# Two steps of a half product taken together per tile, and later transposes of queries and keys, in a two-layer encoder

## The chip, the cores and the metric

The kernel runs on one core of one Trainium2 chip. The metric is the device time of one execution in microseconds (us). Engines are named as the profile names them: PE is the matrix engine (PEld its weight loads), DVE the vector engine, ACT the scalar engine, POOL the GpSimd engine, SP the engine that here only issues transfers. Each engine takes its own instructions in their order and waits on semaphores for the others.

## The reference

The input is 512 tokens of width 1024. Two layers follow one another. Each normalises its input, multiplies it by one wide matrix, applies an attention with 16 heads of 64, multiplies the result by silu of a gate path and by an output matrix, and adds it to its input.

```python
def reference(x, norm_gain, a_w_in, ...):
    for i in range(DEPTH):                      # 2
        hn = rms_norm(x, norm_gain[i])
        j = i // N_MIXERS
        if i % N_MIXERS == 0:
            y = mixer_a(hn, a_w_in[j], ...)     # layer A
        else:
            y = mixer_b(hn, b_w_in[j], ...)     # layer B
        x = x + y.astype(x.dtype)
    return x

def mixer_a(hn, w_in, w_out, q_gain, k_gain, t5_bias):
    proj = hn @ w_in                            # q, k, v of three groups, and the gate
    for g, (window, dilation) in enumerate(DILATED_PAIRS):
        q = rms_norm(qkv[:, :, g, 0], q_gain[g])
        k = rms_norm(qkv[:, :, g, 1], k_gain[g])
        o, lse = dilated_group_attention(q, k, qkv[:, :, g, 2], ...)
    alpha = jax.nn.softmax(jnp.stack(lses), axis=0)
    y = jnp.sum(alpha[..., None] * jnp.stack(outs), axis=0)
    return (y * jax.nn.silu(gate)) @ w_out
```

Layer A attends in three groups of windows: every token, every 4th and every 16th. Layer B attends in a neighbourhood on a grid of 8 by 64. The change touches layer A alone.

## The kernel before

**Number format.** A factor of a large product is split into a high and a low part, and each step of a product is three matmuls into the same accumulator (`mm3`): high by high, high by low, low by high. In the profile the normalised input is `hn_h` and `hn_l`, the weights `wh` and `wl`.

**Weights.** They are read in a fixed order by transfers (`wraw`, issued by SP and POOL, into 8 buffers). ACT casts each piece of 512 columns to `wh` (6 buffers), POOL or DVE subtracts it to get `wl` (5 buffers); some pieces are first sums of two weight blocks, made by DVE. The generator `steps` hands out a pair `wh`, `wl` per step of a product.

**Chunks.** Layer A runs over 8 chunks hc = 0 to 7 of two heads. From hc=1 on, the queries, keys and values of a chunk come out of seven products of half size (`main_a`) in place of eight: both the tokens and the inner dimension are halved, and four of the seven work on sums and differences, prepared once, of the input (`mix_h`, `mix_l`). One such product (`product`) has KH = 4 steps of the inner dimension and two tiles i = 0, 1 of 128 tokens, each with an accumulator of its own of 128 by 512; in each step it does tile 0's three matmuls and then tile 1's. After the last step of a tile its `evac` reads the accumulator: `put22` subtracts that of the fourth mixed product from `rawq` on DVE. The order in a chunk is: two products on the plain input, with the gate of the chunk before in between; the values of the chunk before (from hc=2 on); four mixed products, n = 0, 1, 3, 2; the normalisation of the raw queries (`normed`); in hc=1 the values of chunk 0; and last a product on the plain input (`put21`) that adds on to the accumulators of the mixed product n=2. So this last product may write a tile only after DVE has read it in `put22`.

**Attention.** The attention of chunk hc is done while the products of the next chunk run. `q_a` transposes `rawq` by PE in four groups of four (first one that makes the keys `k0h`, `k0l`, then the queries `q0h`, `q0l`, then two for `q12`), `k_a` does two groups of `rawk` (for `k12`); ACT and DVE copy each group out of a bank. `attn_a` then computes scores in two halves (`scores(0)`, `scores(1)`, four banks each, in the profile `log`), DVE takes their minima into `p` and `mn`, ACT the exponentials, DVE and transfers (`pt`) transpose them, and `weigh` multiplies them by the values (`o`). The transposes and the scores share four banks, which are used in turn.

**What sets the order.** PE's order is that of the program text as it is generated: `run` draws a matmul group from the main generator (the products) and, when a model clock of PE's own time has passed the time named by the last `yield`, a piece from the side generator (the attention). A number yielded there is a pause in model nanoseconds before the next side piece. The first products of a chunk also carry keys such as `("scored", hc - 1)`, at which the main generator lets the side work run until that point is reached. `chore` slips halves of silu, on DVE, into the steps of products. The orders on DVE, ACT and POOL are set by a scheduler, and may change where PE's order does.

Of the kernel before, what the change touches and what calls it, by code (L numbers as in the profile page):

```python
# [22 lines left out]
P = 128  # L23
# [9 lines left out]
H = S // 2  # L33
KH = KT // 2
# [13 lines left out]
def tile_hybrid_encoder(  # L48
# [284 lines left out]
    def mm3(o, lh, ll, rh, rl, first, last, **kw):  # L333
        matmul(o, lh, rh, start=first, stop=False, **kw)
        matmul(o, lh, rl, start=False, stop=False, **kw)
        matmul(o, ll, rh, start=False, stop=last, **kw)
# [21 lines left out]
    def chore(now):  # L358

        if now and chores and next(chores[0], "end") == "end":  # L360
            chores.pop(0)

    def product(acc, stat, open_, evac, guard=None):


        if open_:
            acc += [ps_acc.tile([P, 512], F32, tag="acc", name="acc") for _ in range(2)]
        for k in range(KH):
            chore(1 <= k < KH - 1)
            if k == KH - 1:  # L370
                yield guard
            h, l = next(wsteps)
            for i in range(2):
                sh, sl = (t[:, P * i : P * i + P] for t in stat(k))
                mm3(acc[i], sh, sl, h, l, open_ and k == 0, k == KH - 1, skip_group_check=True)
                if k == KH - 1:
                    evac(i, acc[i])
                yield

    def project(stat_h, stat_l, n, evac, guard, need=None, after=None):  # L380

# [121 lines left out]
    wsteps = steps()  # L503
    wsteps = chain([next(wsteps)], wsteps)
# [198 lines left out]
    def main_a(hc):  # L703
# [49 lines left out]
            yield from v0_a(hc - 1, ("scored", hc - 1))  # L753
        for n, acc, first, put in ((0, c, True, put_v), (1, b, True, put_u), (3, c, False, put12), (2, b, False, put22)):
            yield "mix", n
            yield from product(acc, mixed(n), first, put, ("q", hc - 1) if n == 0 else None)
        normed(box[2], box[1], 8, "rawq", hc)
        if hc == 1:
            yield from v0_a(hc - 1)
        yield from product(b, hn(KH, H), False, put21)  # L760
        if hc == NHC - 1:
            st["y_h"] = big.tile([P, KT, S], F32R, tag="yh", name="y_h")
            st["y_l"] = big.tile([P, KT, S], F32R, tag="yl", name="y_l")
# [194 lines left out]
    def attn_a(hc):  # L958
# [192 lines left out]
        if hc < NHC - 2:  # L1151
            send = lambda: tc.keep_in_program_order(syn.dma_start(y_d[:, hc, :], gt))
            later_on(3000, send)
            stamp["w", hc] = 0
            yield
            if fill:
                later_on(1500, fill)
            yield 1500
            yield from q_a(hc + 1)
            return  # L1160
        st["tail"], back = y_back(range(2), "tr")
# [392 lines left out]
```

## Time and profile before

| | |
|---|---|
| runs | 835.29, 837.63 and 836.27 us |
| their median | 836.27 us |
| the profiled execution | 834.38 us |
| its span | 832.6 us |
| clock granted to PE over the span | 1.00 |
| PE busy | 820.4 us, 99% |
| DVE, ACT, POOL busy | 629.3, 506.3, 301.1 us |

The span is the time between the first and the last instruction on the profile. A line of a timeline gives start, length, engine, program line, operation, output and inputs, shapes, and the number of instructions put together; brackets at its end give idle time of the engine ahead of it and what ended it. The lengths of PE's matmuls overlap, so distances between their starts are what counts. A line of the list of waits gives the total in us, the number of times and the longest. Most instructions bear line 84, which is that of a helper that records operations, so they are told apart by their names.

### The profile page before, as it was taken

Reading aid. Unit: us, or ns where it says so; the run is one execution under the profiler, and the core shown is the slowest. Engines: PE = TensorE matmul, PEld = TensorE weight load, DVE = VectorE, ACT = ScalarE, POOL = GpSimd, SP = SyncE. Lnnn points to the kernel's source line nnn. Section 1 sums busy time; section 2 is a strip of 40 time slices with the busy share of each in tenths; the row PEclk is TensorE's granted clock in tenths of the full one; section 3 lists DMA queues with packets and bytes.
Section 4 is the critical chain, followed back from the end, with each engine's and each line's share of the span. In section 5 each row is a group of like instructions: output and inputs, shape, how many; then the busy total and the mean of one; then the engine's idle time right before and its main releaser. Section 6 shows DMA issues by size and latency. Waiting matters only on the chain.

```text
span 832.6 us, 18133 instructions
## 1 busy us (share of the span) xinstructions
PE 820.4 (99%) x6610; PEld 684.6 (82%) x6610; DVE 629.3 (76%) x1653; ACT 506.3 (61%) x1066; POOL 301.1 (36%) x259
## 2 busy tenths in 40 slices
PE   9999999999999999999999999999999999999998
PEld 7777878878877878878878877789998899989786
DVE  6998997897896886886886867657578777876642
ACT  8566766846846846846846828645366654666440
POOL 4173343543543443543543514312133322333301
PEclk9999999999999999999999999999999999999999
DMA  9427765676686775775676664283354456544212
GB/s 346 138 63 177 187 156 147 137 170 201 129 184 203 161 182 166 160 182 164 156 173 181 134 196 155 81 297 105 99 188 148 124 171 191 165 140 142 87 51 102
DMA packets 55881, 131.97 MB, mean 159 GB/s; under 512 B 6896, under 2 KB 24240, under 8 KB 55664
## 3 DMA queue, kind: packets, MB, share of 16 engines
q1 hardware_dynamic: 49456, 108.40, 41.6%
q0 software_dynamic: 6048, 22.02, 15.1%
q8 instruction: 52, 0.85, 0.4%
q10 hardware_dynamic: 288, 0.39, 0.2%
q14 instruction: 37, 0.30, 0.1%
HBM read 111.73 MB, written 11.72 MB: 148 GB/s over the span
## 4 chain that ended last, share of the span: by engine, by line
PE 87%; ACT 5%; DVE 5%; DMA 2%; issue 2%; POOL 0%; SPq 0%; DVEq 0%; ACTq 0%; POOLq 0%
PE acc L327 72%; PE o L327 5%; PE log L327 5%; PE tp L331 4%; DMA wraw<-in_w 2%; ACT p L84 2%; DVE wl L84 1%; ACT rawk L84 1%; ACT wh L84 1%; DVE rawq L84 1%; DVE rawk L84 0%; ACT sq L84 0%; DVE p L84 0%; DVE ss L84 0%; DVE na L84 0%
## 5 line engine op out<-in xcount | busy, mean ns | idle before, releaser
L84 POOL TENSOR_TENSOR wl<-wraw,wh 128x512 fp32r<-128x512 f32 (+1 forms) x153 | 198.3, 1297 | 401.6 <-PE acc L327 160.7
L84 ACT CAST wh<-wraw 128x512 fp32r<-128x512 f32 (+1 forms) x360 | 208.8, 593 | 179.8 <-PE acc L327 135.3
L84 DVE TENSOR_TENSOR wl<-wraw,wh 128x512 fp32r<-128x512 f32 (+1 forms) x207 | 162.1, 786 | 39.0 <-PE acc L327 24.5
L327 PE MATMUL acc<-wh,hn_h 128*128 128x384 f32 (+1 forms) x488 | 183.9, 378 | 1.3 <-DVE rawq L84 1.2
L327 PE MATMUL acc<-wl,hn_h 128*128 128x384 f32 (+1 forms) x488 | 176.5, 363 | 1.6 <-DVE wl L84 1.6
L327 PE MATMUL acc<-wh,hn_l 128*128 128x384 f32 (+1 forms) x488 | 176.1, 362 | 0.0
L84 ACT ACTIVATE p<-p,mn 128x256 f32<-128x256 f32 (+2 forms) x248 | 138.3, 585 | 23.2 <-DVE mn L84 23.2
L327 PEld LDWEIGHTS acc<-wh,hn_h 128*128 128x128 f32 x488 | 91.9, 189 | 17.1 <-issue 7.0
L327 PEld LDWEIGHTS acc<-wl,hn_h 128*128 128x128 f32 x488 | 91.8, 188 | 10.3 <-DVE wl L84 3.1
L327 PEld LDWEIGHTS acc<-wh,hn_l 128*128 128x128 f32 x488 | 91.6, 188 | 9.6
L327 PE MATMUL acc<-wh,mix_h 128*128 128x512 f32 x224 | 89.0, 397 | 0.0
L327 PE MATMUL acc<-wl,mix_h 128*128 128x512 f32 x224 | 87.4, 390 | 0.0
L327 PE MATMUL acc<-wh,mix_l 128*128 128x512 f32 x224 | 87.3, 390 | 0.0
L327 PE MATMUL acc<-hn_h,wh 128*128 128x512 f32 x192 | 78.2, 407 | 0.0
L327 PE MATMUL acc<-hn_h,wl 128*128 128x512 f32 x192 | 75.1, 391 | 0.0
L327 PE MATMUL acc<-hn_l,wh 128*128 128x512 f32 x192 | 75.1, 391 | 0.0
L84 DVE STREAM_TRANSPOSE pt<-p 128x512 f32<-128x512 f32 (+1 forms) x60 | 40.6, 687 | 23.7 <-ACT p L84 23.5
L327 PE MATMUL acc<-y_h,wh 128*128 128x512 f32 x128 | 51.7, 404 | 0.0
L84 DVE TENSOR_REDUCE ss<-sq 128x4 f32<-128x256 f32 (+1 forms) x96 | 45.5, 497 | 8.2 <-ACT sq L84 4.5
L327 PEld LDWEIGHTS acc<-wh,mix_h 128*128 128x128 f32 x224 | 42.1, 188 | 9.8 <-issue 1.6
L327 PE MATMUL acc<-y_h,wl 128*128 128x512 f32 x128 | 50.0, 390 | 0.0
L327 PE MATMUL acc<-y_l,wh 128*128 128x512 f32 x128 | 50.0, 390 | 0.0
(148 smaller groups left out, 1361.5 us busy)
## 6 DMA issues: line engine op xcount, KB each, us to landing
wraw<-in_w SPq DMA_DIRECT2D x95, 512.0 KB
wraw<-in_w POOLq DMA_DIRECT2D x42, 512.0 KB, 7.3
wraw<-in_w SPq DMA_DIRECT2D x38, 384.0 KB
pt<-pt SPq DMA_DIRECT2D x106, 64.0 KB
td<-tr SPq DMA_DIRECT2D x24, 224.0 KB
pt<-td SPq DMA_DIRECT2D x24, 224.0 KB
e<-l_d SPq DMA_DIRECT2D x32, 112.0 KB
e<-l_d SPq DMA_DIRECT2D x16, 128.0 KB
```

The costliest lines, as they stand in the source:

```text
L84: m = f(*args, **kw)
L327: nc.tensor.matmul(o, l, r, **kw)
L331: nc.tensor.transpose(o, i, ident)
```

## The change

It consists of three edits. `product` gets an argument `two`: a step named there is taken together with the next one, so that tile 0 does both steps, six matmuls, and then tile 1 does both. It is given for the mixed product n=2 (its last two steps) and for the last product (its first two steps). And the pause before the transposes of the next chunk's queries goes from 1500 to 2700 model nanoseconds; that line is passed for hc=0 to 5, so the transposes and first scores of hc=1 to 6 are concerned. With `two`, the pair of weights for both steps is drawn at once, and the last product offers one place for a chore in place of two.

```diff
-    def product(acc, stat, open_, evac, guard=None):
+    def product(acc, stat, open_, evac, guard=None, two=()):
...
-        for k in range(KH):
-            chore(1 <= k < KH - 1)
-            if k == KH - 1:
+        for k0 in range(KH):
+            if k0 - 1 in two:
+                continue
+            ks = (k0, k0 + 1) if k0 in two else (k0,)
+            chore(1 <= k0 < KH - 1)
+            if KH - 1 in ks:
                 yield guard
-            h, l = next(wsteps)
+            ws = [next(wsteps) for _ in ks]
             for i in range(2):
-                sh, sl = (t[:, P * i : P * i + P] for t in stat(k))
-                mm3(acc[i], sh, sl, h, l, open_ and k == 0, k == KH - 1, skip_group_check=True)
-                if k == KH - 1:
-                    evac(i, acc[i])
-                yield
+                for k, (h, l) in zip(ks, ws):
+                    sh, sl = (t[:, P * i : P * i + P] for t in stat(k))
+                    mm3(acc[i], sh, sl, h, l, open_ and k == 0, k == KH - 1, skip_group_check=True)
+                    if k == KH - 1:
+                        evac(i, acc[i])
+                    yield
...
-            yield from product(acc, mixed(n), first, put, ("q", hc - 1) if n == 0 else None)
+            yield from product(acc, mixed(n), first, put, ("q", hc - 1) if n == 0 else None, (KH - 2,) if n == 2 else ())
         normed(box[2], box[1], 8, "rawq", hc)
         if hc == 1:
             yield from v0_a(hc - 1)
-        yield from product(b, hn(KH, H), False, put21)
+        yield from product(b, hn(KH, H), False, put21, None, (0,))
...
-            yield 1500
+            yield 2700
             yield from q_a(hc + 1)
```

How this moves instructions is shown at three places. Numbers behind a name tell buffers apart, and brackets name the engines or queues whose semaphores an instruction waits for.

The first is PE in chunk hc=2, where the mixed product n=2 (inputs `mix_h`, `mix_l`) gives over to the last product (`hn_h`, `hn_l`); `acc_1881` is tile 0 and `acc_1882` tile 1. Before:

```order
L327 MATMUL acc_1881<-wh_1979,mix_h_94 128x512 [waits Activation_49]
L327 MATMUL acc_1881<-wl_1997,mix_h_94 128x512 [waits Pool_49]
L327 MATMUL acc_1881<-wh_1979,mix_l_95 128x512
L327 MATMUL acc_1882<-wh_1979,mix_h_94 128x512
L327 MATMUL acc_1882<-wl_1997,mix_h_94 128x512
L327 MATMUL acc_1882<-wh_1979,mix_l_95 128x512
L327 MATMUL acc_1881<-wh_1995,hn_h_92 128x512 [waits DVE_49,Activation_49]
L327 MATMUL acc_1881<-wl_2009,hn_h_92 128x512
L327 MATMUL acc_1881<-wh_1995,hn_l_93 128x512
```

And with the change:

```order
L327 MATMUL acc_1881<-wh_1979,mix_h_94 128x512 [waits Activation_49]
L327 MATMUL acc_1881<-wl_1997,mix_h_94 128x512 [waits Pool_49]
L327 MATMUL acc_1881<-wh_1979,mix_l_95 128x512
L327 MATMUL acc_1882<-wh_1965,mix_h_94 128x512
L327 MATMUL acc_1882<-wl_1981,mix_h_94 128x512
L327 MATMUL acc_1882<-wh_1965,mix_l_95 128x512
L327 MATMUL acc_1882<-wh_1979,mix_h_94 128x512
L327 MATMUL acc_1882<-wl_1997,mix_h_94 128x512
L327 MATMUL acc_1882<-wh_1979,mix_l_95 128x512
L327 MATMUL acc_1881<-wh_1995,hn_h_92 128x512 [waits DVE_49,Activation_49]
L327 MATMUL acc_1881<-wl_2009,hn_h_92 128x512
L327 MATMUL acc_1881<-wh_1995,hn_l_93 128x512
```

Tile 0's first matmul of the last product stays where it was in the stream, but the last mixed matmul on tile 0 is now six matmuls of tile 1 ahead of it in place of three.

The second is PE in the products of chunk hc=3 where the first group of transposes for `k0h` and `k0l` stands (`tp`); `acc_3019` and `acc_3020` are the tiles of a product, `acc_3144` and `acc_3132` are the gate's accumulator. Before:

```order
L327 MATMUL acc_3019<-wh_2960,hn_l_93 128x512
L331 MATMUL tp_3132<-ident_77,rawq_2683 128x4x32 [waits DVE_49]
L331 MATMUL tp_3132<-ident_77,rawq_2683 128x4x32 x3
L327 MATMUL acc_3020<-wh_2960,hn_h_92 128x512
L327 MATMUL acc_3020<-wl_3005,hn_h_92 128x512
L327 MATMUL acc_3020<-wh_2960,hn_l_93 128x512
```

And with the change:

```order
L327 MATMUL acc_3020<-wh_2960,hn_h_92 128x512
L327 MATMUL acc_3020<-wl_3005,hn_h_92 128x512
L327 MATMUL acc_3020<-wh_2960,hn_l_93 128x512
L327 MATMUL acc_3132<-hn_h_92,wh_3003 128x512 [waits DVE_49,Activation_49]
L327 MATMUL acc_3132<-hn_l_93,wh_3003 128x512
L327 MATMUL acc_3132<-hn_h_92,wl_3024 128x512 [waits DVE_49]
L331 MATMUL tp_3146<-ident_77,rawq_2683 128x4x32 [waits DVE_49]
L331 MATMUL tp_3146<-ident_77,rawq_2683 128x4x32 x3
```

The group stands behind three more matmuls on `acc_3020` and three on the gate, six in all; the groups after it and the first scores move as far.

The third is ACT at the same part of chunks hc=2 and hc=3: casts of weights (`wh`) and copies of the transposed groups. Before, in hc=2:

```order
L84 COPY rawk_155<-acc_2174 128x512 [waits PE_49]
L84 CAST wh_2312<-wraw_1993 128x512 [waits Pool_49]
L84 ACTIVATE k0h_2328<-tp_2331,gk_150 128x512 [waits PE_49]
L84 CAST wh_2340<-wraw_2029 128x512 [waits DMAHW2_49,DVE_49,PE_49]
L84 CAST q0h_2326<-tp_2351 128x512 [waits PE_49]
```

With the change, in hc=2:

```order
L84 COPY rawk_155<-acc_2174 128x512 [waits PE_49]
L84 CAST wh_2312<-wraw_1993 128x512 [waits Pool_49]
L84 CAST wh_2329<-wraw_2029 128x512 [waits DMAHW2_49,DVE_49,PE_49]
L84 ACTIVATE k0h_2338<-tp_2341,gk_150 128x512 [waits PE_49]
L84 CAST q0h_2336<-tp_2357 128x512 [waits PE_49]
```

Before, in hc=3:

```order
L84 CAST wh_3169<-wraw_2844 128x512 [waits DMAHW4_49,DVE_49,PE_49]
L84 COPY q12_3131<-tp_3176 128x512 [waits PE_49]
L84 COPY q12_3131<-tp_3188 128x512 [waits PE_49]
L84 ACTIVATE gt_3197<-acc_3144 128x512 [waits PE_49]
L84 ACTIVATE eg_3198<-gt_3197 128x512 [waits Activation_49]
L84 CAST wh_3205<-wraw_2844 128x512 [waits Pool_49]
L84 ACTIVATE k12_3212<-tp_3213,gk_150 128x512 [waits PE_49]
L84 CAST wh_3223<-wraw_2674 128x512 [waits DMASW2_49,DVE_49,PE_49]
L84 ACTIVATE k12_3212<-tp_3230,gk_150 128x512 [waits PE_49]
```

With the change, in hc=3:

```order
L84 CAST wh_3168<-wraw_2844 128x512 [waits DMAHW4_49,DVE_49]
L84 COPY q12_3145<-tp_3182 128x512 [waits PE_49]
L84 ACTIVATE gt_3191<-acc_3132 128x512 [waits PE_49]
L84 ACTIVATE eg_3192<-gt_3191 128x512 [waits Activation_49]
L84 CAST wh_3199<-wraw_2844 128x512 [waits Pool_49]
L84 COPY q12_3145<-tp_3206 128x512 [waits PE_49]
L84 CAST wh_3216<-wraw_2674 128x512 [waits DMASW2_49,DVE_49,PE_49]
L84 ACTIVATE k12_3223<-tp_3224,gk_150 128x512 [waits PE_49]
L84 CAST wh_3238<-wraw_2674 128x512 [waits PE_49,Pool_49]
L84 ACTIVATE k12_3223<-tp_3245,gk_150 128x512 [waits PE_49]
```

In hc=2 the copy to `k0h` now stands behind one more cast, one that waits for a transfer. In hc=3 one copy to `q12` and both copies to `k12` come later among the casts.

## The prediction

> **What bounds the kernel now.** I read the busy times first, then the chain of waits by engine, then the list of what TensorE (PE) waits for.
>
> ```profile
> span 832.6 us, 18133 instructions
> PE 820.4 (99%) x6610; PEld 684.6 (82%) x6610; DVE 629.3 (76%) x1653; ACT 506.3 (61%) x1066; POOL 301.1 (36%) x259
> PE 87%; ACT 5%; DVE 5%; DMA 2%; issue 2%; POOL 0%; SPq 0%; DVEq 0%; ACTq 0%; POOLq 0%
> PE acc L327 <- DVE wl L84: 1.6, 2, 1.0
> PE acc L327 <- DVE rawq L84: 1.2, 6, 0.2
> PE tp L331 <- DVE k0l L84: 1.0, 1, 1.0
> PE log L327 <- ACT k L84: 0.3, 1, 0.3
> ```
>
> PE works nearly all the span, and the chain that ends last runs through it for 87%. The number of matmuls does not change, so only holes in PE's stream can be won. The last four rows are holes (total us, times, longest): the change aims at the second, six waits for VectorE (DVE) writing `rawq`, and moves work around the last two. The listed 0.2 us is the idle part alone; what a hole costs is read from the distance between starts. Here is the one of chunk hc=2, first PE, then DVE:
>
> ```profile
> 169.32 0.39 PE L327 MATMUL acc<-wh,mix_l 128*128 128x512 f32 x1
> ...
> 170.00 0.39 PE L327 MATMUL acc<-wh,mix_l 128*128 128x512 f32 x1
> 170.58 0.47 PE L327 MATMUL acc<-wh,hn_h 128*128 128x512 f32 x1 [0.19 <-DVE rawq L84]
> 170.89 0.40 PE L327 MATMUL acc<-wl,hn_h 128*128 128x512 f32 x1
> 171.12 0.39 PE L327 MATMUL acc<-wh,hn_l 128*128 128x512 f32 x1
> ...
> 168.00 0.67 DVE L84 TENSOR_TENSOR wl<-wraw,wh 128x512 fp32r<-128x512 f32 x1
> 169.75 1.37 DVE L84 TENSOR_TENSOR rawq<-rawq,acc 128x512 f32<-128x512 f32 x2 [1.07 <-PE acc L327]
> ```
>
> 169.32 is the last matmul on tile 0 of the fourth mixed product, 170.00 the last on tile 1. Undisturbed, starts lie 0.227 us apart (169.32 to 170.00 is three of them). DVE can only begin to read tile 0 at 169.75, each of its two reads takes about 0.69 (1.37 for two), and the last product, which adds on to the same tile, starts at 170.58. From 170.00 to 171.12 there are three starts in 1.12 us instead of 0.68: **0.44 us lost per chunk**.
>
> **The change, part by part.** *Pairing.* No instruction is added. Today tile 0's last mixed matmul and its first matmul of the last product are 4 places apart, 0.91 us, and DVE needs 170.58 − 169.32 = 1.26 us between them. With the two steps taken per tile, tile 1's six matmuls lie between: 7 places, 1.59 us, 0.33 more than is needed. Tile 0 would end at 168.64 (three places earlier), DVE could begin 0.43 later at 169.07, and it is free from 168.67. Tile 1 still ends at 170.00 and comes back after six matmuls of the last product at 171.59; DVE is through with it at 171.12. So the hole closes wholly, for both tiles. The second weight of each pair is wanted three places, 0.68 us, sooner, and the first is held as much longer. The rows that bear on this are GpSimd's (POOL's) subtractions, which make low parts of weights; the second pair of rows is the tightest place that I found, in another product:
>
> ```profile
> 161.39 6.67 POOL L84 TENSOR_TENSOR wl<-wraw,wh 128x512 fp32r<-128x512 f32 x4 [0.97 <-ACT wh L84]
> ...
> 159.12 1.29 POOL L84 TENSOR_TENSOR wl<-wraw,wh 128x512 fp32r<-128x512 f32 x1 [3.37 <-ACT wh L84]
> 160.94 0.39 PE L327 MATMUL acc<-wl,mix_h 128*128 128x512 f32 x1
> ```
>
> The third of POOL's four is the second weight of the mixed pair. At a quarter of 6.67 us each it is there about 166.4 and would be wanted near 168.4, 2 us later; the fourth, the second weight of the last product's pair, is there at 168.06 and wanted beyond 171. At the tight place the low part is ready at 160.41 and used at 160.94, 0.53 us on. A pair with only that would lose 0.68 − 0.53 = 0.15 us a chunk; I take 0, by the pair's own row. Seven chunks take the new order, but in hc=1 another product stands between, and the waits' row counts six. The last of the six:
>
> ```profile
> 481.48 0.39 PE L327 MATMUL acc<-wh,mix_l 128*128 128x512 f32 x1
> 482.06 0.47 PE L327 MATMUL acc<-wh,hn_h 128*128 128x512 f32 x1 [0.19 <-DVE rawq L84]
> ```
>
> Bounds for the pairing: 6 × 0.44 = 2.6 us at the most, and 6 × (0.44 − 0.15) = 1.7 at the least.
>
> *Whether hc=7's share is kept.* Behind the last hole stands a chain that does not start from it:
>
> ```profile
> 470.96 10.08 SPq L84 DMA_DIRECT2D pt<-pt  x16
> 485.87 3.37 SPq L84 DMA_DIRECT2D wraw<-in_w  x4
> ...
> 496.65 0.62 ACT L84 CAST wh<-wraw 128x512 fp32r<-128x512 f32 x1 [10.89 <-DMA wraw<-in_w]
> 505.02 0.40 PE L327 MATMUL acc<-hn_h,wl 128*128 128x512 f32 x1
> 506.40 0.66 PE L331 MATMUL tp<-ident,rawk 128*128 128x128 f32 x4 [0.98 <-DVE k0l L84]
> ```
>
> The weight transfers queue on SP behind the attention's transfers, which began at 470.96, before the hole at 481.48; ScalarE (ACT) stands 10.89 us for one, the keys' norm goes behind it, and PE waits 0.98 us for `k0l` at 506.40. PE arriving 0.44 us sooner waits 0.44 longer. I count five chunks: 5 × 0.44 = **2.2 us** (six if the chain moves along, 2.6).
>
> *The later transposes.* Six times the transposes of queries and keys and the first scores go two steps of six matmuls, 6 × 0.227 = 1.36 us, later; nothing is added on PE, and the second scores stay. What changes is who is late. In hc=3 the first scores now wait:
>
> ```profile
> 260.90 0.30 PE L327 MATMUL log<-k0h,q0h 64*128 64x256 f32 x1
> 261.48 0.38 PE L327 MATMUL log<-k0h,q0h 64*128 64x256 f32 x1 [0.28 <-ACT k L84]
> ...
> 256.48 0.62 ACT L84 CAST wh<-wraw 128x512 fp32r<-128x512 f32 x1 [4.70 <-DMA wraw<-in_w]
> 260.74 0.68 ACT L84 ACTIVATE k<-tp,gk 128x512 f32<-128x512 f32 x1
> ```
>
> A cast waits for its weights until 256.48, and the copies behind it push the keys' second copy to 260.74–261.42; the score is 261.48 − 260.90 = 0.58 us late. Moved, it is wanted at 262.26. In ACT's new order that copy comes one cast (0.62 us) later, ends about 262.0, and lets the score go at 262.06. PE itself comes 0.44 earlier because of the hole before this chunk's scores, while the transfer does not: wanted at 261.82, so some 0.24 still stands. Gain 0.58 − 0.24 = **0.3 us** (bounds 0 and 0.6).
>
> In hc=1 and hc=2 the two copies of the last `rawk` tiles, a sum of squares and a cast come in front of the keys' second copy:
>
> ```profile
> 193.49 0.62 ACT L84 CAST wh<-wraw 128x512 fp32r<-128x512 f32 x1 [3.57 <-DMA wraw<-in_w]
> ...
> 189.23 0.69 ACT L84 ACTIVATE k0h<-tp,gk 128x512 fp32r<-128x512 f32 x1 [1.37 <-PE tp L331]
> 199.81 0.69 ACT L84 ACTIVATE k<-tp,gk 128x512 f32<-128x512 f32 x1
> 201.78 0.42 ACT L84 ACTIVATE sq<-rawk 128x256 f32<-128x256 f32 x1
> ...
> 197.31 0.60 PE L331 MATMUL tp<-ident,rawk 128*128 128x128 f32 x4
> 201.47 0.30 PE L327 MATMUL log<-k0h,q0h 64*128 64x256 f32 x2
> ```
>
> The second copy, 199.81 with 0.69 us now, takes the place of the last square, 201.78 to 202.47; wanted at 201.47 + 1.36 = 202.83, or 202.39 after the hole's 0.44. I price hc=2 at 0.1 us and hc=1 at 0.1 (bounds 0 and 0.5 each): −0.2. In hc=2 the cast that stands 3.57 us for its transfer also comes ahead of `k0h`, which moves from 189.2 to about 194.0; `k0l` would follow near 195.5, ahead of the keys' transposes (197.3 now, 198.7 then) that want its bank. That hides it by some 3 us; each us beyond would stop PE.
>
> That ACT holds everything behind a waiting instruction is also what the Trainium skill says ("TensorE: Matmul & The Clock Gate", under Architectural detail): its queue is strict first-in first-out, unlike PE's, which pulls weight loads ahead. By that rule no later copy can pass the cast at 193.49, and the trace agrees (the copy of `q0h` starts at 194.01, though the cast waited 3.57 us).
>
> *Second scores.* They want the banks of the first, which DVE must have read:
>
> ```profile
> 141.34 0.41 DVE L84 TENSOR_REDUCE ss<-sq 128x4 f32<-128x256 f32 x1
> 143.83 0.48 DVE L84 CUSTOM_DVE_ANT_1 p<-log,e,mn 128x256 f32<-128x256 f32 x1
> ...
> 146.33 0.25 PE L327 MATMUL log<-k0h,q0h 64*128 64x192 f32 x2
> ```
>
> In hc=1 the last read ends at 144.31 and its bank is wanted at 146.33: 2.0 us. The shift takes 1.36 and leaves 0.65; the sum of squares that now stands between the reads (141.34, 0.41 us) goes in front of them, which adds nothing to the last one's end. I charge nothing; the bound is rival C.
>
> **Sum.** 2.2 + 0.3 − 0.2 = 2.3 us, between 0.4 (five pairs at 0.29, nothing in hc=3, 0.5 lost in each of hc=1 and 2) and 3.2 (2.6 and 0.6). The profiled execution took 834.38 us (span 832.6 and 1.78 around it): 832.1 expected of its like. The median of the runs shown is 836.27, 1.9 above it; so the forecast is 836.27 − 2.3 = **834.0 us**. What a measurement can tell from no change is 0.3%, 2.5 us, so this sits at that bound.
>
> The skill's figure for the warm distance of 512-column matmuls ("TensorE: Matmul & The Clock Gate", section Back-to-back issue gap) is 0.216 us; this trace has 0.227 at a granted clock of 1.000. By the page the hole would be 1.12 − 0.65 = 0.47 us, 2.4 instead of 2.2 for five. I use the row.
>
> **Rivals.**
>
> *A, more than the sum.* With PE's holes gone in every chunk, the chain of hc=7 also begins earlier, hc=3's wait closes wholly and a few reads that DVE does after a hole come sooner: 2.6 + 0.6 and another 0.5 to 1 in holes (the two of 1.6 us for `wl` are far from here, which speaks against). Time: about 832.5.
>
> *B, a new wait takes the old one's place.* Transposes later by 1.36 us leave ACT's key copies, the softmax's reads and the weights in hc=1 and 2 (0.53 us ahead, above) with little. If the six chunks lose 0.3 each, 1.8 of the 2.3 is gone: 835.8. For it: the 0.24 in hc=3 and margins of 0.3 in hc=1 and 2. Against: in hc=4 to 6 ACT is not held by a transfer there.
>
> *C, slower: the shorter gap between the two scores decides.* The second scores wait on DVE's reads of the first. The spare 2.0 us of hc=1 becomes 0.65; if DVE's queue does a weight sum (1.23 us) and a subtraction (0.69 us) ahead of the reads, or waits there as here in hc=6,
>
> ```profile
> 443.91 1.23 DVE L84 TENSOR_TENSOR wraw<-wraw 128x1024 f32<-128x1024 f32 x1 [3.05 <-DMA wraw<-in_w]
> 445.05 0.69 DVE L84 TENSOR_TENSOR wl<-wraw,wh 128x512 fp32r<-128x512 f32 x1
> ```
>
> the wait is 1.92 − 0.65 = 1.27 us, and six of them are 7.6 less 2.3, +5.3: 841.6. It decides once DVE is over 0.65 us later than PE's shift. For it: DVE is 76% busy, more than ACT. Against: in the new order only the sum of squares comes in front of the reads of hc=1 and 2.
>
> *D, no effect.* The pairing does not close the hole, DVE being late for tile 0 with something else: by the row at 168.00 it is free 0.4 us before. The time stays at 836.3.
>
> **How the numbers follow.** The sum as worked out has a chance of 0.50, its own range 833.1 to 835.9; A 0.14; B 0.20; C 0.08; D 0.08. The sum lies on the bound, so a good half of its chance, 0.30, counts as faster by over 0.3% and 0.20 as no change; A is faster; B and D are no change but for 0.02 that ends slower; C is slower. Faster 0.44, within 0.3% 0.46, slower 0.10. The range takes in A, the sum, B and D and leaves out C: 832.0 to 837.0.
>
> **What would show it.** Right: the six waits for `rawq` gone from the list; from tile 1's last mixed matmul the next start 0.23 us later; the wait for `k` in hc=3 at most half; the wait for `k0l` near 1.4 us instead of 1.0. Wrong: waits of `log` for ACT `k` in hc=1 or 2, or for DVE `mn` or `p` at the second scores (C); waits for `wl` or `wh` inside the pairs; a span that falls by more than 3.2 us, whose place I would then not have seen.

## The result, and the profile after

The changed kernel takes 848.15 us (median of 6 runs, 844.75 to 851.9). The kernel before takes 836.67 us beside it (6 runs, 834.26 to 838.03, the three shown above among them). The ratio is 1.0151 [1.0132, 1.017]: **slower by 1.5%**, where 834.0 us, 0.3% faster, had been forecast, with a range up to 837.0. In the two profiled executions the spans are 849.2 and 832.6 us, 16.6 us apart; that of the changed kernel took 850.96 us, 2.8 above its median. The order of work is read from these, and the prices are taken from medians. Two executions of the experiments, of 1347.67 and 2011.87 us, were in a slow state and are left out of the medians and ratios below.

The head of the page of the changed kernel with its chain of waits, and then the list of what its PE waits for:

```profile
span 849.2 us, 18124 instructions
PE 828.4 (98%) x6610; PEld 689.2 (81%) x6610; DVE 644.7 (76%) x1653; ACT 504.6 (59%) x1066; POOL 309.7 (36%) x259
PE 47%; DMA 4%; ACT 4%; DVE 2%; issue 1%; SPq 1%; POOL 1%; POOLq 0%; ACTq 0%; DVEq 0%
```

```profile
PE log L327 <- ACT k L84: 4.1, 7, 0.7
PE acc L327 <- POOL wl L84: 3.0, 5, 0.9
PE tp L331 <- DVE k0l L84: 1.7, 1, 1.7
...
PE tp L331 <- DVE gt L84: 1.3, 1, 1.3
```

The six waits for `rawq` are gone, as meant. The first scores now wait seven times for ACT's copies of the keys, where there was one such wait, and new are five waits for low parts of weights from POOL and one for `gt`. The share of PE in the chain has nearly halved, with DMA and SP's queue (SPq) now in it. The hole of the transition between the mixed product n=2 and the last product is closed; on PE's timeline in chunk hc=2 it now reads:

```profile
172.04 0.39 PE L327 MATMUL acc<-wl,mix_h 128*128 128x512 f32 x1
172.26 0.39 PE L327 MATMUL acc<-wh,mix_l 128*128 128x512 f32 x1
172.49 0.39 PE L327 MATMUL acc<-wh,hn_h 128*128 128x512 f32 x1
```

The next start follows 0.23 us after tile 1's last mixed matmul, where it was 0.58. So the loss lies elsewhere. I measured it by the stretch from the start of one chunk's second scores to the next one's, which PE's timeline gives (the chunk named is the one at the stretch's end; us):

| kernel | hc=1 | 2 | 3 | 4 | 5 | 6 | 7 |
|---|---|---|---|---|---|---|---|
| before | 54.1 | 62.2 | 62.8 | 62.1 | 62.2 | 62.2 | 60.7 |
| after | 54.7 | 64.4 | 64.2 | 64.7 | 63.5 | 68.6 | 62.4 |
| pair_only | 54.6 | 63.4 | 63.2 | 62.6 | 62.6 | 62.6 | 60.1 |
| delay_only | 54.1 | 63.6 | 63.4 | 62.6 | 62.7 | 63.8 | 64.3 |
| delay_half | 54.2 | 62.3 | 63.2 | 63.5 | 63.2 | 66.9 | 64.1 |
| delay_one | 54.2 | 62.2 | 62.2 | 66.2 | 62.2 | 62.7 | 60.7 |
| pair_sq_gt | 54.7 | 61.9 | 63.1 | 61.8 | 61.8 | 63.1 | 60.9 |
| bias_later | 54.15 | 62.15 | 62.17 | 62.17 | 62.17 | 62.17 | 59.91 |
| pair_sq_gt_bias | 54.63 | 61.69 | 61.69 | 61.69 | 61.69 | 61.69 | 59.81 |
| all_bias_later | 54.7 | 63.3 | 62.8 | 62.0 | 61.9 | 61.9 | 62.6 |

The first two rows differ by 16.0 us in sum, which is nearly all of the 16.6. It comes in every chunk, the largest part in hc=6. The other rows are the experiments, told below. In chunk hc=4 the first scores of the changed kernel look like this on PE:

```profile
329.59 0.78 PE L327 MATMUL log<-k0h,q0h 64*128 64x192 f32 x2
...
331.12 0.38 PE L327 MATMUL log<-k0h,q0h 64*128 64x256 f32 x1 [0.54 <-ACT k L84]
...
332.22 0.38 PE L327 MATMUL log<-k0h,q0h 64*128 64x256 f32 x1 [0.71 <-ACT k L84]
...
333.88 0.50 PE L327 MATMUL acc<-wh,hn_h 128*128 128x512 f32 x1
```

The block takes 333.88 − 329.59 = 4.29 us; undisturbed it takes 2.00 (the row of 75 score matmuls below). By the same distance the first scores lose 1.40, 2.30, 1.20 and 3.62 us in hc=3 to 6, and 0.52 in hc=7. That is about half of the 16.0 us; the kernel before lost 0.66 so, in hc=3. No second scores lost anything in any kernel of this study.

Behind it stands a chain over SP's queue and ACT. The changed kernel, SP and then ACT:

```profile
304.33 12.33 SPq L84 DMA_DIRECT2D e<-l_d  x6
316.82 2.99 SPq L84 DMA_DIRECT2D wraw<-in_w  x3
...
326.70 0.62 ACT L84 CAST wh<-wraw 128x512 fp32r<-128x512 f32 x1 [5.82 <-DMA wraw<-in_w]
331.47 0.70 ACT L84 ACTIVATE k<-tp,gk 128x512 f32<-128x512 f32 x1
```

And the kernel before at the same place, SP, then the start of its first scores on PE, and then the whole block as a row of its chain of waits:

```profile
296.28 7.63 SPq L84 DMA_DIRECT2D e<-l_d  x6
304.08 5.25 SPq L84 DMA_DIRECT2D wraw<-in_w  x3
```

```profile
323.26 0.36 PE L327 MATMUL log<-k0h,q0h 64*128 64x192 f32 x2
```

```profile
323.33 2.00 PE log L327 x75
```

The six transfers `e` are the attention bias of the next chunk (`bias_a`). In SP's queue they stand behind the transfers `pt` and ahead of the weights. PE reaches the scores 6.33 us later than before (329.59 and 323.26), but the weights are issued 12.74 us later (316.82 and 304.08). So ACT's cast waits for its weight, the key copies stand behind it, and PE waits for them.

### The profile page after: what moved, and what is told of

It is laid out like the page before. It is cut to its first block, busy times and chain, and to the rows that moved or that the text cites. A ratio compares the mean times of both kernels' runs of the same rounds, so it can differ in the third digit from the quotient of the medians.

```text
span 849.2 us, 18124 instructions
## 1 busy us (share of the span) xinstructions
PE 828.4 (98%) x6610; PEld 689.2 (81%) x6610; DVE 644.7 (76%) x1653; ACT 504.6 (59%) x1066; POOL 309.7 (36%) x259
## 4 chain that ended last, share of the span: by engine, by line
PE 47%; DMA 4%; ACT 4%; DVE 2%; issue 1%; SPq 1%; POOL 1%; POOLq 0%; ACTq 0%; DVEq 0%
PE acc L327 40%; DMA wraw<-in_w 3%; PE o L327 3%; PE log L327 3%; PE tp L331 2%; ACT p L84 1%; SPq L84 1%; DMA e<-l_d 1%; ACT wh L84 1%; DVE p L84 1%; ACT rawk L84 1%; DVE wl L84 1%; POOL wl L84 0%; ACT y_h L84 0%; ACT k L84 0%
## 5 line engine op out<-in xcount | busy, mean ns | idle before, releaser
L84 POOL TENSOR_TENSOR wl<-wraw,wh 128x512 fp32r<-128x512 f32 (+1 forms) x153 | 208.9, 1369 | 394.5 <-ACT wh L84 157.3
L84 ACT CAST wh<-wraw 128x512 fp32r<-128x512 f32 (+1 forms) x360 | 206.6, 593 | 158.5 <-PE acc L327 104.1
L84 DVE TENSOR_TENSOR wl<-wraw,wh 128x512 fp32r<-128x512 f32 (+1 forms) x207 | 167.7, 814 | 35.3 <-PE acc L327 20.6
L327 PEld LDWEIGHTS acc<-wl,mix_h 128*128 128x128 f32 x224 | 42.1, 188 | 14.2 <-POOL wl L84 4.9
```

The source lines that it names most:

```text
L84: m = f(*args, **kw)
L327: nc.tensor.matmul(o, l, r, **kw)
```

## The experiments

After the result I had three theories. **P**: the pairing itself costs, since it moves weights and ACT's work. **D**: the later transposes cost, through ACT and the weights. **Q**: a loop over SP's queue (softmax, `pt`, bias, weights, casts, key copies, next scores) turns any lateness into more lateness. The expectations call P the pair theory and Q the loop theory; D is not set apart in them. Ratios are against the kernel before, in the same group of runs (835.92, 835.55, 835.28 and 835.22 us in the four groups).

**The two halves alone.** *pair_only* is the changed kernel with the old pause; *delay_only* is the kernel before with the new one.

```diff
 # pair_only, from after
-            yield 2700
+            yield 1500
 # delay_only, from before
-            yield 1500
+            yield 2700
```

> The change with the pause before the query transposes put back to 1500, so only the two steps are taken together per tile. Loop theory (the later pause moves the first scores, with them the softmax, SP's queue of attention transfers, the weight transfers behind it, ACT's cast and the next chunk's scores, until this loop is longer than PE's work): the six waits for rawq are gone, 5 to 6 times 0.44 us are won, 834.0 to 834.6 beside 836.7. Pair theory (drawing two weights at once and holding the first longer makes the weights late, as the new waits for POOL's wl say): 845 to 850, as with the whole change.

> The kernel before with the pause alone at 2700, no steps taken together. Loop theory: slower by 12 to 17 us, 849 to 853, with SP's first attention transfer 1.4 us or more later behind the end of the chunk before's first scores plus its own loss in every chunk from hc=3 on, and waits of the scores for ACT's k. Pair theory: 836 to 838.

pair_only took 838.79 us, ratio 1.003 [1.002, 1.004]; delay_only 843.28, 1.0083 [1.0066, 1.0101]. The sum of both, 2.87 + 7.36 = 10.2 us, is near to the 11.5 of the whole change. So the loss is nearly additive, and **the larger part comes from the later transposes**. Neither time lies in a range that was expected of it: each half costs something, and neither costs all. PE's longest waits in pair_only, and then those in delay_only:

```profile
PE tp L331 <- DVE gt L84: 4.2, 5, 1.5
```

```profile
PE tp L331 <- DVE k0l L84: 2.7, 1, 2.7
PE acc L327 <- POOL wl L84: 2.7, 5, 0.8
```

The pairing closes its hole and opens another: the first transposes of `rawq` take over a bank of the weighted values `o`, and have to wait until DVE has multiplied these by the gate (`gt`). Before, DVE and PE at that place:

```profile
187.71 0.87 DVE L84 TENSOR_TENSOR gt<-gt,o 128x128 f32<-128x128 f32 x4
...
188.60 0.60 PE L331 MATMUL tp<-ident,rawq 128*128 128x128 f32 x4
```

DVE ends at 188.58 and PE starts at 188.60: a margin of nothing, which no list of waits shows. In pair_only, on ACT, DVE (two rows) and PE:

```profile
172.55 0.62 ACT L84 CAST wh<-wraw 128x512 fp32r<-128x512 f32 x1 [1.01 <-PE acc L327]
...
173.74 0.69 DVE L84 TENSOR_REDUCE ss<-sq 128x8 f32<-128x512 f32 x1 [1.34 <-ACT sq L84]
...
189.56 0.87 DVE L84 TENSOR_TENSOR gt<-gt,o 128x128 f32<-128x128 f32 x4
...
189.90 0.66 PE L331 MATMUL tp<-ident,rawq 128*128 128x128 f32 x4 [1.47 <-DVE gt L84]
```

Weights are drawn in pairs, so ACT has a cast more ahead of the second square of `rawq`, and this cast waits 1.01 us for PE, for a buffer which the pair holds longer. DVE waits 1.34 us for the square, its norm is late, and what follows on DVE, down to `gt`, is late with it.

In delay_only the cast and the subtraction behind the second scores are late in hc=1 and 2. Here hc=1, first before and then delay_only (ACT, POOL, PE):

```profile
158.43 0.61 ACT L84 CAST wh<-wraw 128x512 fp32r<-128x512 f32 x1
```

```profile
159.91 0.61 ACT L84 CAST wh<-wraw 128x512 fp32r<-128x512 f32 x1
...
160.61 1.27 POOL L84 TENSOR_TENSOR wl<-wraw,wh 128x512 fp32r<-128x512 f32 x1 [2.48 <-ACT wh L84]
...
161.93 0.50 PE L327 MATMUL acc<-wl,mix_h 128*128 128x512 f32 x1 [0.83 <-POOL wl L84]
```

The softmax starts from the first scores, so the exponentials on ACT, with this cast among them, shift by the 1.4 us of the change. The margin of 0.53 us, which the prediction quoted for this very subtraction, is overrun.

**A shorter pause.** An earlier place for the transposes takes the key copies out of the way, but should make the wait for `gt` longer. *pair_900* is the changed kernel with this pause:

```diff
-            yield 2700
+            yield 900
```

> The change with the pause at 900 in place of 2700, so the query and key transposes and the first scores come earlier than before. Loop theory: the loop gets slack, the wait of hc=3's scores for ACT's k (0.58 us by starts) shrinks or goes, and the time is that of the pairing alone or up to 0.6 us less, 833.4 to 834.6. Against it: if the normalised rawq or a bank is not ready so early, PE waits at the transposes instead, one wait of up to 0.7 us in each of six chunks, 838.

It took 841.89 us, 1.0059 [1.0043, 1.0076], above both times that were expected, with `gt` as its one large wait, and no first score waiting:

```profile
PE tp L331 <- DVE gt L84: 8.0, 6, 2.2
```

So the pause stands between two limits, `gt` ahead and the key copies behind, and at 1500 it is near both.

**The bias off SP's queue.** *late_e_on_pool* is the whole change, with the bias of the chunks from hc=2 on issued by POOL:

```diff
+        queue = pol if hc > 1 else syn
...
-            syn.dma_start(
+            queue.dma_start(
```

> The whole change, but from hc=3 on the six transfers of the bias e per chunk are issued by POOL's queue and no longer stand on SP's queue between the attention's transfers and the weights. Loop theory: SP's weight transfers behind them start 5 to 12 us sooner, ACT's longest wait for a weight transfer (12.5 us) falls, and 8 us or more of the 11.5 us lost come back, 836 to 841. If the loss is in the softmax or in ACT's own order and not in SP's queue: 846 to 850.

(By the edit this starts with the bias of hc=2, not of hc=3.) It took 846.3 us, 1.0118 [1.0092, 1.0145], which is in the range expected if SP's queue were not the cause. None of the first scores waited, which speaks for Q, but other waits took their place, these above all:

```profile
PE acc L327 <- POOL wl L84: 3.1, 9, 0.8
PE acc L327 <- DVE rawq L84: 1.3, 6, 0.3
```

POOL also makes the low parts of weights, and nine of these now come late in place of five. And the six waits for `rawq` are back: with the other order on DVE the pairing's hole is open again. So this run changed more than the place of the bias in SP's queue, and decides nothing about it.

**The second square ahead of the cast, and half the delay.** *pair_sq_first* issues the second square at once, not after other ACT work; *all_sq_first* is the same in the whole change. *delay_half* is the kernel before with a pause of 2100, and *pair_sq_first_half* is pair_sq_first with it.

```diff
 # in put22: pair_sq_first (pause 1500), all_sq_first (2700), pair_sq_first_half (2100)
-            squares_soon(t, box[1], 2 + i, 8)
+            (squares if i else squares_soon)(t, box[1], 2 + i, 8)
 # delay_half, from before
-            yield 1500
+            yield 2100
```

> The steps taken together, pause 1500, and one thing more: the square of tile 1 of the fourth mixed product is put on ACT at once and not after a delay, so it stands ahead of the two casts that the last product's pair draws. Cast theory (the pair holds weight buffers longer, a cast waits for its buffer, the square waits behind the cast, DVE's sum of squares 1.34 us behind that, the keys' norm and the product with gt after it, and the first transposes for gt's bank): the waits of tp for gt go from 4.2 us to under 1, the 0.37 us won at each of six transitions stays, 833.0 to 834.8 beside about 836. If gt is late for another reason (DVE's evacuation of the paired tiles itself): 837.5 to 839, as with the pairing alone.

> The whole change with the pause at 2700 and the same square put first. If the two parts only add up and the square cures the pairing: the delay's 7.4 us less 2.2, 840 to 842. If the loop from the first scores over softmax, SP's transfers and ACT's cast bounds the kernel whatever the norm does: 845 to 849.

> The kernel before with the pause at 2100: transposes and first scores one group of three matmuls pairs later, 0.68 us in place of 1.36. Margin theory (the weights behind the second scores have 0.52 us to spare in hc=1 and 2 and lose what the softmax is later beyond that; the same for the keys at the end): 0.16 us in some five places and 0.7 at the end of hc=7, less 0.6 for hc=3's scores: 836 to 838. If any shift costs in proportion: half of 7.4, 839 to 840.

> The steps taken together, the square first, and the pause at 2100. Margin theory: 833.5 to 836, since the transitions' 2.2 us stay and the shift of 0.68 us is mostly spare. In proportion: 837 to 838.

| kernel | us | ratio |
|---|---|---|
| pair_sq_first | 836.71 | 1.0008 [0.9993, 1.0023] |
| all_sq_first | 845.71 | 1.0112 [1.0074, 1.0149] |
| delay_half | 844.48 | 1.009 [1.0065, 1.0116] |
| pair_sq_first_half | 846.61 | 1.0123 [1.0095, 1.0152] |

The square's place is more than half of the pairing's cost: the `gt` waits fall from 4.2 to 1.5 us, and the time is 1.2 us above the kernel before of its group, where pair_only's was 2.9. But now the first scores lose 1.73 and 1.19 us in hc=3 and hc=6, so nothing is won. And **half of the delay costs as much as the whole** (844.48 and 843.28), where 836 to 838 was expected of a sum of margins and at most 840 of a cost in proportion. In delay_half nothing is lost in hc=2, then about 1 us a chunk, 4.7 in hc=6 and 3.4 in hc=7. Part of this is the halved clock that is told at the end: at a granted clock of 1.000 each kernel has one run, and these took 840.82 and 843.27 us.

**`gt` ahead of the keys' norm, and the delay in a single chunk.** *gt_early* puts the norm of the raw keys 2500 model nanoseconds later, so that `gt` comes before it on DVE. *pair_gt_early* is pair_only with it, *pair_sq_gt* pair_sq_first with it. *delay_one* delays the transposes of hc=3 alone.

```diff
 # gt_early (in normed), also in pair_gt_early and pair_sq_gt
+        elif held[0] and key == "rawk" and 1 < hc < NHC - 1:
+            def known():
+                st[key, hc] = raw
+                stamp[key, hc] = clock[0]
+
+            later_on(2200, known)
+            later_on(2200 + 2500, lambda: head_norm(raw, ss, ns, False))
 # delay_one, from before
-            yield 1500
+            yield 2700 if hc == 2 else 1500
```

> The kernel before with only the keys' norm put 2500 model ns later. Gt theory: nothing waits for gt before, so nothing is won: 835.5 to 837. If the later norm itself costs (the keys' transposes wait for rawk): 838 or more.

> Steps taken together, pause 1500, and on DVE the norm of the keys of hc=2 to 6 put 2500 model ns later, so that the four products of the attention's output with gt, which free the banks for the transposes, stand ahead of the norm's eleven small operations and not behind them. PE's order is that of the pairing alone. Gt theory (the pairing's loss is the wait of the first transposes for gt, which stands behind a norm that is late): the 4.2 us of waits for gt go, the transitions' 2.2 us stay won: 833.5 to 835 beside about 836. If the transposes then wait for rawq or the scores for a late k instead: 836 to 839.

> The same with the square of tile 1 put first on ACT as well. Gt theory: 833.0 to 834.8, the hc=2 wait of 1.8 us by starts that the square alone left is gone; what is left is the wait of the scores for ACT's k in hc=3 and hc=6, about 1 us each. If the norm was what held things up: no more than the square alone, 836.7.

> The kernel before with the pause at 2700 for one chunk, the transposes and first scores of hc=3 alone, 1.36 us later. Loop theory (softmax, SP's transfers, ACT's cast and the next chunk's key copies are counted from the first scores, with 0.4 us to spare in hc=4): hc=3's own wait of 0.58 us goes, hc=4's scores wait about 1 us, later chunks little: 836 to 837.5. If a later pause costs its own chunk and only that: hc=3's weights behind the second scores late by about 1 us, hc=4's scores unchanged.

| kernel | us | ratio |
|---|---|---|
| gt_early | 835.69 | 0.9999 [0.9987, 1.0012] |
| pair_gt_early | 837.62 | 1.0023 [1.001, 1.0036] |
| pair_sq_gt | 836.34 | 1.001 [0.9998, 1.0022] |
| delay_one | 836.89 | 1.0012 [0.9998, 1.0027] |

gt_early by itself changes nothing. Added to the pairing it leaves 2.8 of the 4.2 us of waits for `gt`, and its ratio of 1.0023 cannot be told from the 1.003 of pair_only. With both cures (pair_sq_gt) the pairing has no wait for `gt` left, and still gains nothing. The pairing's stretches in hc=2, 4 and 5 are 0.3 to 0.4 us shorter than before, but hc=3 and hc=6 take 63.1, with the first scores waiting. delay_one's time is not clear of no change, but its profiled execution shows how such a wait comes about: with hc=3 delayed, it is **hc=4** whose first scores wait, though its own transposes are where they were. On PE:

```profile
324.16 0.38 PE L327 MATMUL log<-k0h,q0h 64*128 64x256 f32 x1 [0.68 <-ACT k L84]
325.26 0.39 PE L327 MATMUL log<-k0h,q0h 64*128 64x256 f32 x1 [0.71 <-ACT k L84]
```

The stretch to hc=4 took 66.2 us in place of 62.1; the one to hc=3 became 0.6 shorter (its score wait was gone, as forecast). So lateness of one chunk's first scores reappears a chunk later, over a loop. Its first half can be read from SP's first `pt` of the attention of hc=4, before and then after:

```profile
346.59 0.60 SPq L84 DMA_DIRECT2D pt<-pt  x1
```

```profile
356.35 0.60 SPq L84 DMA_DIRECT2D pt<-pt  x1
```

From the end of the first scores (325.26, 333.88) that is 21.3 and 22.5 us. In hc=3 to 6 this distance is 21.3 to 21.5 us in every kernel with a pause of 1500, but for delay_one, where it is 22.3 in the delayed hc=3 and 21.8 in hc=4. It is 22.2 to 22.8 in delay_only, and 23.3 to 24.4 in delay_half. So a delay comes back by more than its own size, and half of it makes this part of the loop longer than the whole does, which fits that it costs no less. The other half is the part of SP's queue shown above; where first scores wait, the whole turn takes longer than the 62.2 us that PE needs for a chunk. P and D name where lateness starts, and Q what becomes of it. Whether Q holds can be told by taking the bias out of the loop without loading another engine.

**The bias behind the weights.** *bias_later* is the kernel before, with the bias of the next chunk issued after `weigh`, as it is in hc=0 already. On SP the weights then stand ahead of the six `e`. *pair_sq_gt_bias* is pair_sq_gt with it, *all_bias_later* the whole change with it.

```diff
-        if hc:
-            st["e", hc + 1] = bias_a(hc + 1)
         yield "wait", ("pt", hc), (0, 11500)[hc] if hc < 2 else 9000 if hc == NHC - 2 else 7500
         yield "wait", ("gate", hc), 4000
         gt = weighed(hc, (yield from weigh()))
-        if not hc:
-            st["e", hc + 1] = bias_a(hc + 1)
+        st["e", hc + 1] = bias_a(hc + 1)
```

> The kernel before with the six transfers of the bias e of the next chunk issued after the attention's output and not before it, so on SP they stand behind two or three weight transfers that they were ahead of. PE's and ACT's orders are unchanged. Loop theory: ACT's cast in hc=3 gets its weights 4 us or more sooner, the 0.66 us of hc=3's first scores go: 834 to 835 beside 835.5. Rival (softmax and ACT's order): the excess of hc=3's scores stays, 835 to 836.5.

> Steps taken together, square first, keys' norm behind gt, and the bias transfers later. Loop theory: the excesses of 1.4 us each at the first scores of hc=3 and hc=6 go and the transitions' 2.2 us are kept: 832.5 to 834. Rival: the excesses stay, 836 to 837.

> The whole change with the bias transfers later. Loop theory: the excesses of the first scores (1.4, 2.3, 1.2 and 3.6 us in hc=3 to 6) go; what is left is the weights behind the second scores (five times about 0.9), gt in hc=2 and the keys in hc=7: 838 to 842. Rival: 846 to 850.

| kernel | us | ratio |
|---|---|---|
| bias_later | 832.61 | 0.9969 [0.9956, 0.9981] |
| pair_sq_gt_bias | 831.27 | 0.9955 [0.9942, 0.9967] |
| all_bias_later | 838.15 | 1.0036 [1.0023, 1.005] |

SP's queue ahead of hc=3's scores, before and then in bias_later:

```profile
236.23 10.15 SPq L84 DMA_DIRECT2D e<-l_d  x6
246.54 2.71 SPq L84 DMA_DIRECT2D wraw<-in_w  x3
```

```profile
235.67 1.45 SPq L84 DMA_DIRECT2D wraw<-in_w  x3
237.16 11.82 SPq L84 DMA_DIRECT2D e<-l_d  x6
```

The weights go 10.9 us sooner (246.54 and 235.67). ACT's waits for them, before and in all_bias_later, where even the whole change leaves next to nothing:

```profile
ACT wh L84 <- DMA wraw<-in_w: 23.9, 6, 10.9
```

```profile
ACT wh L84 <- DMA wraw<-in_w: 1.0, 2, 0.8
```

In all three kernels the first scores of hc=1 to 6 lose no time any more; those of hc=7 lose 0.53 us. The first two are faster than either of their ranges, the third lies in the loop theory's. The unchanged kernel gains 2.6 us from this edit: its score wait in hc=3 and its wait for `k0l` in hc=7 are gone. The whole change costs 838.15 − 832.61 = 5.5 us with the bias behind the weights, and 11.5 with it ahead. So **about 6 of the 11.5 us went through the bias's place in the loop**, as Q has it (what the halved clock behind late scores cost is among them), and the other 5.5 are left to P and D. And the pairing, with its two cures, now gains what it was forecast to: the stretches to hc=2 to 6 are 61.69 us in place of 62.17 (62.15 in hc=2), 0.48 a chunk. In the chain of waits of pair_sq_gt_bias, the second scores of hc=2, 3 and 6 start at

```profile
207.59 1.98 PE log L327 x75
...
269.27 1.98 PE log L327 x75
...
454.33 1.98 PE log L327 x75
```

that is 61.68 us apart in the first pair, and 3 × 61.69 in the second.

The 2.4 us of the five are not all kept: the stretch to hc=1 is 0.48 longer, where PE waits as much longer for ACT's `vt`, and the medians of the two kernels differ by 1.3. pair_sq_gt_bias is the fastest kernel of the study, 0.45% below the kernel before. What all_bias_later still loses against it lies mostly in the stretches to hc=2, 3 and 7 (1.6, 1.1 and 2.8 us by the table): in each of the first two a low part of a weight is late by 0.83 us, and in the third `k0l` by 1.59.

## Why the prediction was wrong

**What bounds the kernel**: right. PE did, and holes were what counted. But the list of waits shows only margins that are already overrun. That some stood at nothing (`gt` at 188.58 against 188.60) was in the timeline; the prediction went by the waits listed alone.

**Pairing, the hole**: right in mechanism and size. The next start is at 0.23 us, tile 1's return is free too, and with the loop's slack restored a chunk is 0.48 us shorter where 0.44 was worked out.

**Pairing, "I take 0, by the pair's own row"**: this is the step that failed on the pairing's side. I priced only whether the second weight of a pair is ready in time. What it cost was elsewhere: the pair's other weight holds its buffer longer, the additional cast on ACT waits 1.01 us for a buffer, and the square behind it carries DVE's order up to `gt` with it. Measured: +2.9 us where −2.2 was forecast; the square's place explains 1.7 of it (pair_sq_first), and with the norm's place changed too the last `gt` waits are gone (pair_sq_gt).

**The later transposes, "nothing is added on PE", 0.3 − 0.2 us**: this is the step that failed most, +7.4 us by itself. Three terms of it:

- *hc=3, "while the transfer does not" move.* A loss of 0.24 us was to be left there; the first scores of the changed kernel lose 1.40. The weight's arrival at 256.48 was taken as given. It hangs on the previous chunk's first scores, through softmax, `pt`, bias and weights in SP's queue. So the same shift that makes PE later makes the weight later a chunk on. This is where the sum had no term at all. bias_later's row, weights at 235.67 in place of 246.54, and the 6 us of the whole change that go with the bias's place show it.
- *hc=1 and 2, 0.1 us each.* The margins of key copies were about right: there the first scores lost nothing in the changed kernel. But the exponentials shift with the first scores, and the cast between them too (158.43 to 159.91). The margin of 0.53 us at that subtraction, which I quoted, went into the sum with the pairing alone; it belonged to the delay, for which only rival B named it. The hole there is 1.22 us between starts where 0.23 is undisturbed: 1.0 us a chunk.
- *hc=4 to 6, "ACT is not held by a transfer there".* For hc=5 this was wrong before already: at the same place of the chunk ACT stood 4.02 us for a weight's transfer ahead of the cast at 380.79, nearly as long as in hc=3, and only no first score was late by it. After, a cast stood 5.82 us in hc=4 (326.70), 4.73 in hc=5 and 5.99 in hc=6.

Nor had the sum a term for the clock, which was taken as 1.00 throughout: the holes in the first scores of hc=6 were followed by a halved one (below).

**hc=7**: right that the wait for `k0l` grows (1.0 to 1.7 us; forecast 1.4), but not for the reason given: in pair_only, where the hole of the transition is closed too, it is 0.9. I took its chain as fixed; by the delay alone the wait grows to 2.7, and with the bias behind the weights the kernel before has no such wait, so it hangs on the same queue.

**Second scores, rival C**: right to leave at nothing. No second score lost time in any kernel; the mechanism of my only slower rival was not the one. **Rival B** had the place right (ACT's key copies, the softmax and the weights of hc=1 and 2) and the price wrong: 0.3 us a chunk, where the changed kernel's stretches of hc=2 to 6 are 1.3 to 6.4 us longer. It was priced as an overrun of one margin, and without the loop.

**The chances**: slower had 0.10, all of it on C and the tail of B and D. A loop with little slack should have been a rival of its own; the row that spoke for it (the cast's 4.70 us wait in hc=3) stood in the prediction.

What stays open: why the six bias transfers take 7.6 us of SP's queue in one chunk and 12.3 in another, why in several kernels hc=6 loses most, and why the way from the first scores to the first `pt` is longest with half of the delay. That the loop passes lateness on is shown; its exact gain per turn was not measured.

## What to carry to other kernels

Before you move work later, follow each thing that hangs on it once round all engines and queues until you are back at PE, and compare the length of that loop with the chunk: if it has no slack, a small shift costs again in each chunk, and a list of waits of the kernel before says little about it. Look for releases with a margin of nothing (the end of one row against the start of another), not only for waits. In a transfer queue shared by several uses, put what the next casts want ahead of what is needed later: here that change of order alone gave 2.6 us, and made the gain of the pairing show.

## What the runs showed of the chip that I had not expected

**The clock granted to PE was halved behind short holes among narrow matmuls.** Windows of the changed kernel around the first scores of hc=6 (columns: window, its length, busy time and count of PE, PEld, DVE, ACT, POOL, then the granted clock, DMA share and GB/s), and then two rows of PE's timeline a little later:

```profile
459.00:461.00 2.00, 0.96 (x6) 0.59 (x6) 2.00 (x3) 2.00 (x5) 1.23 (x2) 1.00 0.07 29
...
462.00:467.00 5.00, 5.00 (x74) 3.81 (x73) 3.80 (x12) 1.85 (x5) 1.74 (x2) 0.50 0.50 83
```

```profile
465.21 0.63 PE L327 MATMUL acc<-wh,hn_l 128*128 128x512 f32 x1
465.64 0.63 PE L327 MATMUL acc<-hn_h,wh 128*128 128x512 f32 x1
```

PE was never idle for more than 0.71 us at a stretch there, but was busy only 0.96 of 2 us. After that the clock was 0.50 for 6.8 us, and matmuls started 0.43 us apart in place of 0.227. The same came in delay_one behind the rows of 324.16 and 325.26, and in delay_half at hc=6. In the profiled execution of the changed kernel it cost an estimated 2.8 us: about 8 matmuls of the product at twice their distance (1.7 us), and some 1.1 in the scores themselves. Of the six runs the one with a mean clock of 1.000 was the fastest (844.75 us), and the one with 0.990 the slowest (851.9). In hc=4, where the first scores lost 2.30 us, the clock stayed at 1.00. The Trainium skill ("TensorE: Matmul & The Clock Gate", section HAM oscillation — how this bites in real kernels) tells of a drop to half when PE waits across an activity window of more than 3.4 us. The trace agrees on the half, but no idle time here was near that length, so one long idle stretch is not needed. Nor is a low busy share always enough: in pair_sq_first_half PE waited 3.17 us for `k0l` in hc=7, was busy 0.26 of the 3 us from 517 to 520, and kept a clock of 1.00. What decides, no run here tells.

**A small DVE operation lasted as long as a subtraction on POOL.** In pair_only, DVE and POOL at the same time, and then the same operation before:

```profile
174.68 1.60 DVE L84 TENSOR_SCALAR rs<-nv 128x32 int32<-128x32 int32 x1
...
174.63 1.60 POOL L84 TENSOR_TENSOR wl<-wraw,wh 128x512 fp32r<-128x512 f32 x1
```

```profile
173.49 0.18 DVE L84 TENSOR_SCALAR rs<-nv 128x32 int32<-128x32 int32 x1
```

0.18 us became 1.60, and both ended within 0.05 us of one another. The norm of the kernel before has such a row too, one of 1.17 us at 175.06, which ends within 0.05 us of a subtraction on POOL. The Trainium skill ("SBUF — State Buffer", section Who interferes with whom) says that DVE in some of its modes and GpSimd take turns at a shared pair of ports for a whole instruction. These rows agree with that, but I made no run to show it. If it is so, the time of a small operation on DVE depends on what POOL does at that moment, and a row of before is not its price once the order moves.
